# A gated hybrid decoder block: the root's scale and epsilon inside its square root, the last chunk squared on VectorE, one of the last four multiplications on GpSimd

## The chip, the cores and the metric

The kernel runs on one core of a Trainium2 chip. The metric is the device time of one execution in microseconds (us), given as the median of several runs; the kernel before has 1648.81 us as the median of three (1648.59 to 1650.45).

## The reference

One decoder block of width 2048 on 256 tokens, in float32. Three parts are added to the residual x one after the other, each on an RMS-normalised copy of it, and the result is normalised once more:

```python
def rms_norm(x, g):
    y = x * lax.rsqrt(jnp.mean(x * x, axis=-1, keepdims=True) + EPS)
    return y * g

x = x + hybrid_mixer(rms_norm(x, g_mix), w_in, ..., w_out)
x = x + memory_cross_attention(rms_norm(x, g_cross), rms_norm(mem, g_mem), w_cq, w_ckv, w_co)
x = x + conv_glu_ffn(rms_norm(x, g_ffn), w_up, conv_w, conv_b, w_down)
return rms_norm(x, g_final)
```

The mixer merges gated linear attention and causal pooling by sigmoid gates. Nearly all arithmetic is products of the 256 tokens with weight matrices (312 MB of weights are read). What matters here is the five times repeated `rsqrt(mean(x*x) + EPS)`: for the mixer's input, for the memory and the cross attention's input, for the feed-forward input, and for the output.

## The kernel before

Tokens lie along the free dimension, the 2048 channels as 16 chunks of 128 partitions. Each weight tile is loaded by SyncE's DMA queue into a `raw` buffer, cast by ScalarE into a high part `wh` (line 110), and VectorE writes the rest `wl` as the difference (line 110). TensorE then makes two products for each tile in three terms. Up to three units of weights are prepared ahead (`LOOK`), in five buffers for `wh`, five for `wl` and six for `raw`. A scheduler gives each engine a fixed order of instructions; `behind` and `issue_after` put a small step behind a named matmul. Engines wait for each other by semaphores; an engine that waits holds back all that is queued behind on it. In the lists of instructions, `[waits DVE_49]` means that the instruction waits for VectorE.

A norm is made in three steps. `Sum` adds up squares (`acc`). `cols` sums them over the partitions by a matmul with ones into a small PSUM tile `cps` and calls `root`, whose result `rc` is the reciprocal root with one Newton step. `rows` puts `rc` on a diagonal (`diag`) and spreads it over the partitions by another matmul (`rps`). The PSUM tiles `cps` and `rps` come from the pool `aux`, which has four buffers handed out in turn. The square root has its own table of ScalarE (the ACT_TABLE_LOAD in front of line 292).

At the start (mixer, values and decay gates) `va_unit` makes the products of lines 403 to 405. The units of the second half (n = 1) accumulate in four tiles of the pool `aux`: `va_0_560`, `va_1_561`, `va_0_562` and `va_1_563`. The tile `cps_mix` is allocated between the first tile of that pool (`warm`) and these four, so that the fourth of them, `va_1_563`, lies in the buffer of `cps_mix` and can be written when the last reader of `cps_mix` is done.

At the end, the last six chunks of the down projection are made for tokens 0 to 127 first (lines 922, 923), then for tokens 128 to 255 (line 928). `tail_out` adds the two halves of the product to x (line 891), squares on ScalarE (893), adds the square to `acc` on VectorE (896), and for the last chunk hands the square itself to `tail_norm`, which sums it by a matmul of its own (903). `tail_norm` makes the root, the diagonal (907), the spreading matmul (909), and then four multiplications of 128x512 on VectorE (912), each followed by its store on SyncE's queue (913). The first token half runs under the matmuls of the second; the second half is alone at the end.

Of the kernel before, what the change touches and what calls it, by code (L numbers as in the profile page):

```python
# [8 lines left out]
F32 = mybir.dt.float32  # L9
F32R = mybir.dt.float32r  # L10
U32 = mybir.dt.uint32
AF = mybir.ActivationFunctionType
# [3 lines left out]
P = 128  # L16
T = 256
D = 2048
NC = D // P
# [123 lines left out]
def block(ctx, tc, xT, memT, vecs, masks, wa2, wpool, w_va, w_in, w_branch, w_out, w_ckv_k, w_ckv_v, w_cq, w_co, w_up, w_down, out):  # L143
    nc = tc.nc
# [8 lines left out]
    sm = ctx.enter_context(tc.tile_pool(name="sm", bufs=2))  # L153
# [32 lines left out]
    def xc(c):  # L186
        return x[c // 4][:, c % 4, :]
# [23 lines left out]
    eps_t = const.tile([P, 1], F32, name="eps_t")  # L211
# [39 lines left out]
    class Sum:  # L251
# [18 lines left out]
        def cols(self):  # L270

            ps = aux.tile([P, 2], F32, tag="aux", name=f"cps_{self.name}")
            for t in range(2):
                nc.tensor.matmul(ps[:, t : t + 1], lhsT=self.acc[:, t * P : (t + 1) * P], rhs=ones[:, 0:1], start=True, stop=True)
            return root(ps, 2, self.name)
# [12 lines left out]
    def root(ps, n, name):  # L288

        v, y, z, r = (const.tile([P, n], F32, name=f"rc{i}_{name}") for i in range(4))  # L290
        nc.vector.tensor_scalar(v, ps, 1.0 / D, EPS, ALU.mult, ALU.add)
        nc.scalar.activation(y, v, AF.Sqrt)
        nc.vector.reciprocal(y, y)
        nc.vector.tensor_mul(z, y, y)
        nc.vector.scalar_tensor_tensor(z, z, -0.5, v, ALU.mult, ALU.mult)
        nc.vector.scalar_tensor_tensor(r, z, 1.5, y, ALU.add, ALU.mult)
        return r
# [13 lines left out]
    def gemm(unit, act, name, n=NC):  # L311

        ps = mm.tile([P, 2 * T], F32, tag="mm", name=f"ps_{name}")
        products(ps, terms(W.get(unit), act, n))
        return ps
# [27 lines left out]
    def total(ps, name):  # L343

        t = sm.tile([P, T], F32, tag="ev", name=f"ev_{name}", bufs=3)
        nc.scalar.copy(t, ps[:, T : 2 * T])
        u = sm.tile([P, T], F32, tag="eu", name=f"eu_{name}", bufs=3)
        nc.vector.tensor_add(u, ps[:, 0:T], t)
        return u
# [32 lines left out]
    v = [big.tile([P, HEADS, T], F32, tag="u", name=f"v{t}") for t in range(2)]  # L382
# [277 lines left out]
    for m in range(NC):  # L660
        wps = W.get(br0 + m)
        ys = []
        for n in (1, 0):
            ps = mm.tile([P, 2 * T], F32, tag="mm", name=f"br{m}_{n}")
            products(ps, [(wps[n], k, og if n == 0 else op, k) for k in range(8)])
            y = total(ps, f"br{m}_{n}")
# [32 lines left out]
    for m in range(NC):  # L699
        ps = gemm(ck0 + m, me, f"ck{m}")  # L700
# [170 lines left out]
    def scale_last(m, t=None):  # L871
        ts = slice(0, 2) if t is None else slice(t, t + 1)
        nc.scalar.activation(y_fin[m // 4][:, ts, m % 4, :], halves(xc(m))[:, ts, :], AF.Identity, scale=col(V_FINAL, m))
# [14 lines left out]
    def tail_out(m, t, ps):  # L888
        xt = xc(m)[:, t * P : (t + 1) * P]
        for g in range(2):  # L890
            nc.vector.tensor_add(xt, xt, ps[:, g * T + t * P : g * T + (t + 1) * P])
        sq = sm.tile([P, P], F32, tag="sq", name=f"sqt{m}_{t}", bufs=3)
        nc.scalar.activation(sq, xt, AF.Square)
        if m < NC - 1:
            a = s_z.acc[:, t * P : (t + 1) * P]
            nc.vector.tensor_add(a, a, sq)
            scale_last(m, t)
        return sq

    def tail_norm(t, sq):  # L900
        ps = aux.tile([P, 1], F32, tag="aux", name=f"cps_fin{t}")
        nc.tensor.matmul(ps, lhsT=s_z.acc[:, t * P : (t + 1) * P], rhs=ones[:, 0:1], start=True, stop=False)
        nc.tensor.matmul(ps, lhsT=sq, rhs=ones[:, 0:1], start=False, stop=True)
        rc = root(ps, 1, f"fin{t}")
        scale_last(NC - 1, t)
        diag = sm.tile([P, P], F32, tag="sq", name=f"diag_fin{t}", bufs=3)
        nc.vector.tensor_scalar(diag, ident, rc, None, ALU.mult)
        ps = aux.tile([P, P], F32, tag="aux", name=f"rps_fin{t}")
        nc.tensor.matmul(ps, lhsT=ones, rhs=diag, start=True, stop=True)
        for i in range(4):  # L910
            y = y_fin[i][:, t]
            nc.vector.tensor_mul(y, y, ps[:, None, :].to_broadcast([P, 4, P]))
            nc.sync.dma_start(out[t, :, 4 * i : 4 * i + 4, :], y)

    tails = []
    for m in range(NC - TAIL, NC):
        pool, tag = (aux, "aux") if m >= NC - 2 else (mm, "mm")
        ps = pool.tile([P, 2 * T], F32, tag=tag, name=f"ps_dt{m}")
        ts = terms(W.get(down0[2] + m), ga[2], n_last)
        products(ps, ts[:1], last=False)  # L920
        for (hi, lo), k, act, c in ts[1:]:
            nc.tensor.matmul(fours(ps[:, 0:T]), lhsT=lo[:, k * P : (k + 1) * P], rhs=fours(act.hi(c)), start=False, stop=False, skip_group_check=True)
            nc.tensor.matmul(of_tokens(ps, 0), lhsT=hi[:, k * P : (k + 1) * P], rhs=of_tokens(act.both(c), 0), start=False, stop=False, skip_group_check=True)
        sq = tail_out(m, 0, ps)
        tails.append((m, ps, ts))
    for n, (m, ps, ts) in enumerate(tails):
        for i, ((hi, lo), k, act, c) in enumerate(ts[1:]):
            pe["last"] = nc.tensor.matmul(of_tokens(ps, 1), lhsT=hi[:, k * P : (k + 1) * P], rhs=of_tokens(act.both(c), 1), start=False, stop=i == n_last - 2, skip_group_check=True)
        if n == 0:
            behind(tail_norm, 0, sq)  # L930
        sq1 = tail_out(m, 1, ps)
    tail_norm(1, sq1)


# [53 lines left out]
```

## Time and profile before

| | |
|---|---|
| median of 3 runs | 1648.81 us |
| profiled execution, its own time | 1650.06 us |
| its span in the profile | 1648.3 us |
| TensorE busy | 1635.4 us (99%) |
| VectorE busy | 1227.9 us (74%) |
| ScalarE busy | 899.4 us (55%) |
| GpSimd busy | 31.1 us (2%) |
| granted TensorE clock, mean | 0.998 |

The times in the rows below count from the span's start. The profiled execution took 1.76 us more than its span. PE is TensorE's matmuls, PEld its weight loads, DVE VectorE, ACT ScalarE, POOL GpSimd, SPq the issuing of DMAs on SyncE.

### The profile page before, as it was taken

Reading aid. Unit: us, or ns where it says so; the run is one execution under the profiler, and the core shown is the slowest. Engines: PE = TensorE matmul, PEld = TensorE weight load, DVE = VectorE, ACT = ScalarE, POOL = GpSimd, SP = SyncE. Lnnn points to the kernel's source line nnn. Section 1 sums busy time; section 2 is a strip of 40 time slices with the busy share of each in tenths; the row PEclk is TensorE's granted clock in tenths of the full one; section 3 lists DMA queues with packets and bytes.
Section 4 is the critical chain, followed back from the end, with each engine's and each line's share of the span. In section 5 each row is a group of like instructions: output and inputs, shape, how many; then the busy total and the mean of one; then the engine's idle time right before and its main releaser. Section 6 shows DMA issues by size and latency. Waiting matters only on the chain.

```text
span 1648.3 us, 26006 instructions
## 1 busy us (share of the span) xinstructions
PE 1635.4 (99%) x9900; PEld 1474.9 (89%) x9900; DVE 1227.9 (74%) x1906; ACT 899.4 (55%) x1376; POOL 31.1 (2%) x137
## 2 busy tenths in 40 slices
PE   8999999999999999999999999999999999999997
PEld 8999998989988898889999999999999999999987
DVE  7588768677888855447777788886678887678876
ACT  7555447445556644446555565654356664446563
POOL 2000000000001100000000000000000000000000
PEclk9999999999999999999999999999999999999999
DMA  8665556656666666665446666666666666666663
GB/s 275 208 200 171 168 166 189 218 169 201 195 220 210 196 199 196 192 194 177 154 144 199 194 195 200 196 200 196 199 196 198 198 196 200 195 201 194 180 183 109
DMA packets 90734, 316.15 MB, mean 192 GB/s; under 512 B 10208, under 2 KB 11104, under 8 KB 90608
## 3 DMA queue, kind: packets, MB, share of 16 engines
q1 hardware_dynamic: 90464, 314.43, 61.2%
q8 instruction: 77, 1.26, 0.3%
q14 instruction: 49, 0.40, 0.1%
q10 hardware_dynamic: 144, 0.05, 0.0%
HBM read 312.35 MB, written 2.10 MB: 191 GB/s over the span
## 4 chain that ended last, share of the span: by engine, by line
PE 97%; DMA 1%; DVE 1%; ACT 1%; issue 0%; SPq 0%; DVEq 0%; ACTq 0%
PE ps_up L329 19%; PE ps_up L330 10%; PE ps_g L329 7%; PE ps_dn L329 7%; PE ps_dn L330 4%; PE ps_g L330 4%; PE ps_wc L329 3%; PE ps_ck L329 3%; PE ps_cq L329 3%; PE br L329 3%; PE ps_wo L329 3%; PE ps_cq L330 2%; PE br L330 2%; PE ps_wc L330 2%; PE ps_ck L330 2%; PE cv L722 2%
## 5 line engine op out<-in xcount | busy, mean ns | idle before, releaser
L110 ACT CAST wh<-raw 128x1024 fp32r<-128x1024 f32 (+3 forms) x602 | 613.1, 1021 | 652.4 <-issue 204.1
L110 DVE TENSOR_TENSOR wl<-raw,wh 128x1024 fp32r<-128x1024 f32 (+3 forms) x602 | 718.2, 1195 | 331.9 <-ACT wh L110 322.2
L329 PE MATMUL ps_up<-h,wh 128*128 128x512 f32 x1408 | 469.9, 380 | 0.0
L330 PE MATMUL ps_up<-h,wl 128*128 128x256 f32 x1408 | 386.4, 274 | 0.0
L329 PEld LDWEIGHTS ps_up<-h,wh 128*128 128x128 f32 x1408 | 264.3, 188 | 45.3
L330 PEld LDWEIGHTS ps_up<-h,wl 128*128 128x128 f32 x1408 | 264.5, 188 | 0.0
L329 PE MATMUL ps_g<-h,wh 128*128 128x512 f32 x512 | 173.3, 384 | 0.0
L329 PE MATMUL ps_dn<-ga,wh 128*128 128x512 f32 x512 | 170.8, 380 | 0.0
L330 PE MATMUL ps_g<-h,wl 128*128 128x256 f32 x512 | 140.6, 275 | 0.0
L330 PE MATMUL ps_dn<-ga,wl 128*128 128x256 f32 x512 | 140.5, 274 | 0.0
L329 PEld LDWEIGHTS ps_g<-h,wh 128*128 128x128 f32 x512 | 96.2, 188 | 16.8 <-ACT wh L110 0.2
L329 PEld LDWEIGHTS ps_dn<-ga,wh 128*128 128x128 f32 x512 | 96.1, 188 | 16.5
L330 PEld LDWEIGHTS ps_g<-h,wl 128*128 128x128 f32 x512 | 96.2, 188 | 0.3 <-issue 0.2
L330 PEld LDWEIGHTS ps_dn<-ga,wl 128*128 128x128 f32 x512 | 96.2, 188 | 0.0
L329 PE MATMUL ps_wo<-mg,wh 128*128 128x512 f32 x256 | 87.2, 386 | 0.1
L329 PE MATMUL ps_cq<-h,wh 128*128 128x512 f32 x256 | 86.3, 382 | 0.0
L329 PE MATMUL ps_wc<-oc,wh 128*128 128x512 f32 x256 | 85.9, 381 | 0.0
L329 PE MATMUL ps_ck<-me,wh 128*128 128x512 f32 x256 | 85.9, 382 | 0.0
L330 PE MATMUL ps_wo<-mg,wl 128*128 128x256 f32 x256 | 70.4, 276 | 0.0
L330 PE MATMUL ps_ck<-me,wl 128*128 128x256 f32 x256 | 70.3, 274 | 0.0
L330 PE MATMUL ps_cq<-h,wl 128*128 128x256 f32 x256 | 70.3, 274 | 0.0
L330 PE MATMUL ps_wc<-oc,wl 128*128 128x256 f32 x256 | 70.1, 275 | 0.0
(322 smaller groups left out, 2747.2 us busy)
## 6 DMA issues: line engine op xcount, KB each, us to landing
raw<-w_up SPq DMA_DIRECT2D x176, 512.0 KB, 4.1
raw<-w_in SPq DMA_DIRECT2D x112, 512.0 KB, 3.9
raw<-w_down SPq DMA_DIRECT2D x64, 512.0 KB, 4.3
raw<-w_branch SPq DMA_DIRECT2D x32, 512.0 KB, 4.3
raw<-w_out SPq DMA_DIRECT2D x32, 512.0 KB, 4.1
raw<-w_ckv_k SPq DMA_DIRECT2D x32, 512.0 KB, 3.9
raw<-w_ckv_v SPq DMA_DIRECT2D x32, 512.0 KB, 4.3
raw<-w_cq SPq DMA_DIRECT2D x32, 512.0 KB, 4.4
```

The costliest lines, as they stand in the source:

```text
L110: return self.nc.scalar.copy(hi, src), self.nc.vector.tensor_sub(lo, src, hi.bitcast(F32))
L329: nc.tensor.matmul(fours(ps), lhsT=wh, rhs=fours(act.both(c)), start=f, stop=False, skip_group_check=True)
L330: pe["last"] = nc.tensor.matmul(fours(ps[:, 0:T]), lhsT=wl, rhs=fours(act.hi(c)), start=False, stop=l, skip_group_check=True)
L722: nc.tensor.matmul(fours(acc[t]), lhsT=xh, rhs=fours(wl), start=False, stop=False)
```

## The change

There are three edits.

In `root`, the square root reads the sums in PSUM directly, with the scale 1/D and the epsilon (the constant tile `eps_t`) as its own scale and bias. The value v = sum/D + EPS is still made on VectorE, since the Newton step needs it. `root` is called for all five norms.

In `tail_out`, the square of the last chunk (m = 15) is made on VectorE instead of ScalarE.

In `tail_norm`, ScalarE copies the spread factors `rps` from PSUM to a tile r in SBUF; GpSimd multiplies the first quarter of the output by r, and ScalarE's queue stores it; VectorE multiplies the other three quarters, the second one first, and SyncE's queue stores these.

```diff
     def root(ps, n, name):
         v, y, z, r = (const.tile([P, n], F32, name=f"rc{i}_{name}") for i in range(4))
+        nc.scalar.activation(y, ps, AF.Sqrt, bias=eps_t, scale=1.0 / D)
         nc.vector.tensor_scalar(v, ps, 1.0 / D, EPS, ALU.mult, ALU.add)
-        nc.scalar.activation(y, v, AF.Sqrt)
         nc.vector.reciprocal(y, y)
...
         sq = sm.tile([P, P], F32, tag="sq", name=f"sqt{m}_{t}", bufs=3)
-        nc.scalar.activation(sq, xt, AF.Square)
+        if m < NC - 1:
+            nc.scalar.activation(sq, xt, AF.Square)
+        else:
+            nc.vector.tensor_mul(sq, xt, xt)
...
-        for i in range(4):
+        r = sm.tile([P, P], F32, tag="eu", name=f"r_fin{t}", bufs=3)
+        nc.scalar.copy(r, ps)
+        for i in (1, 0, 2, 3):
             y = y_fin[i][:, t]
-            nc.vector.tensor_mul(y, y, ps[:, None, :].to_broadcast([P, 4, P]))
-            nc.sync.dma_start(out[t, :, 4 * i : 4 * i + 4, :], y)
+            by, eng, queue = (r, nc.gpsimd, nc.scalar) if i == 0 else (ps, nc.vector, nc.sync)
+            eng.tensor_mul(y, y, by[:, None, :].to_broadcast([P, 4, P]))
+            queue.dma_start(out[t, :, 4 * i : 4 * i + 4, :], y)
```

The edits change the order in which instructions stand. The first place is VectorE in the root of the mixer's norm. `wl_0_569` is the low part of a weight tile of the third unit of the second half; `rc_mix` stands for the four small tiles of the root, of which line 291 before and line 292 now write v.

```order
 L110 TENSOR_TENSOR wl_1_491<-raw_1_485,wh_1_490 128x780 [waits DMAHW5_49,PE_49,Activation_49]
-L291 TENSOR_SCALAR rc_mix<-cps_mix 128x2 [waits PE_49]
-L110 TENSOR_TENSOR wl_0_569<-raw_0_564,wh_0_568 128x780 [waits DMAHW0_49,Activation_49]
-L293 RECIPROCAL rc_mix<-rc_mix 128x2 [waits Activation_49]
+L110 TENSOR_TENSOR wl_0_569<-raw_0_564,wh_0_568 128x780 [waits DMAHW0_49,PE_49,Activation_49]
+L292 TENSOR_SCALAR rc_mix<-cps_mix 128x2 [waits Activation_49]
+L293 RECIPROCAL rc_mix<-rc_mix 128x2
```

The instruction that writes v stood in front of `wl_0_569` and waited for TensorE. It now stands behind it and waits for ScalarE, whose square root reads the same PSUM tile.

The second place is TensorE in the first unit of the second half, with the four accumulators named above.

```order
 L405 MATMUL va_0_562<-wl_0_453,h_147 128x260
-L403 MATMUL va_1_563<-wh_0_452,h_147 128x260 [waits DVE_49]
-L404 MATMUL va_1_563<-wh_0_452,h_147 128x260
-L405 MATMUL va_1_563<-wl_0_453,h_147 128x260
 L403 MATMUL va_0_560<-wh_0_452,h_147 128x260
...
 L405 MATMUL va_1_561<-wl_0_453,h_147 128x260
 L403 MATMUL va_0_562<-wh_1_454,h_147 128x260 [waits Activation_49]
+L403 MATMUL va_1_563<-wh_0_452,h_147 128x260 [waits DVE_49]
+L404 MATMUL va_1_563<-wh_0_452,h_147 128x260
+L405 MATMUL va_1_563<-wl_0_453,h_147 128x260
```

The three matmuls that first write `va_1_563` stand seven matmuls later than before (three on `va_0_560`, three on `va_1_561`, one on `va_0_562`). The first of them still waits for VectorE.

The third place is VectorE at the very end, in the second token half. `x_92` holds the last four chunks, `y_9549` to `y_9551` are the second to the fourth quarter of the output.

```order
+L899 TENSOR_TENSOR acc_fin<-acc_fin,sqt_1_16951 128x128 [waits Activation_49]
 L891 TENSOR_TENSOR x_92<-x_92,ps_dt_16813 128x128 [waits PE_49]
-L896 TENSOR_TENSOR acc_fin<-acc_fin,sqt_1_16949 128x128 [waits DVE_49,Activation_49]
 L891 TENSOR_TENSOR x_92<-x_92,ps_dt_16813 128x128 [waits DVE_49]
...
+L896 TENSOR_TENSOR sqt_1_16968<-x_92 128x128 [waits DVE_49]
+L292 TENSOR_SCALAR rc_fin_16973<-cps_fin_16970 128x1 [waits Activation_49]
+L293 RECIPROCAL rc_fin_16974<-rc_fin_16974 128x1
...
+L918 TENSOR_TENSOR y_9549<-y_9549,rps_fin_16986 128x512 [waits Activation_49]
+L918 TENSOR_TENSOR y_9550<-y_9550,rps_fin_16986 128x512
+L918 TENSOR_TENSOR y_9551<-y_9551,rps_fin_16986 128x512
```

The sum of chunk 14 stands before both additions of chunk 15 instead of between them, v is written after ScalarE's square root, and the first multiplication waits for ScalarE, which copies the same `rps` to r. Before, the first multiplication waited for TensorE alone.

## Rows read from the trace of the kernel before

**Rows 1.** Page, part 1: busy time of each engine, share, instructions

```profile
PE 1635.4 (99%) x9900; PEld 1474.9 (89%) x9900; DVE 1227.9 (74%) x1906; ACT 899.4 (55%) x1376; POOL 31.1 (2%) x137
```

**Rows 2.** Waits of TensorE: total us, times, longest

```profile
PE rps_fin L909 <- DVE diag_fin L907: 1.7, 1, 1.7
...
PE va L403 <- DVE rc_mix L291: 0.6, 1, 0.6
```

**Rows 3.** Windows: stretch, its length, busy PE PEld DVE ACT POOL, PEclk, DMA share, GB/s

```profile
36.00:1638.40 1602.40, 1602.32 (x9665) 1444.17 (x9663) 1196.39 (x1844) 872.42 (x1320) 21.65 (x105) 1.00 0.61 190
```

**Rows 4.** Timeline at the mixer's root: start us, duration us, engine, line, operation

```profile
33.68 0.28 PE L404 MATMUL va<-wh,h 128*128 128x260 f32 x1
33.80 0.28 PE L405 MATMUL va<-wl,h 128*128 128x260 f32 x1
34.46 0.15 DVE L291 TENSOR_SCALAR rc_mix<-cps_mix 128x2 f32<-128x2 f32 x1
...
34.67 0.39 PE L403 MATMUL va<-wh,h 128*128 128x260 f32 x1 [0.59 <-DVE rc_mix L291]
...
35.02 0.85 ACT L110 CAST wh<-raw 128x780 fp32r<-128x780 f32 x1 [1.81 <-DMA raw<-w_va]
...
35.89 1.28 ACT L292 ACT_TABLE_LOAD   x1
35.90 0.97 DVE L110 TENSOR_TENSOR wl<-raw,wh 128x780 fp32r<-128x780 f32 x1 [1.28 <-ACT wh L110]
...
37.18 0.20 ACT L292 ACTIVATE rc_mix<-rc_mix 128x2 f32<-128x2 f32 x1
```

**Rows 5.** Timeline at the feed-forward norm's root

```profile
940.16 1.23 DVE L110 TENSOR_TENSOR wl<-raw,wh 128x1024 fp32r<-128x1024 f32 x1 [0.19 <-ACT wh L110]
...
941.62 0.59 PE L283 MATMUL rps_wc<-diag_wc,ones 128*128 128x256 f32 x2
```

**Rows 6.** Timeline of the end

```profile
1638.45 0.29 DVE L891 TENSOR_TENSOR x<-x,ps_dt 128x128 f32<-128x128 f32 x1 [0.32 <-PE ps_dt L928]
...
1638.86 0.28 DVE L891 TENSOR_TENSOR x<-x,ps_dt 128x128 f32<-128x128 f32 x1
1639.24 0.31 ACT L893 ACTIVATE sqt<-x 128x128 f32<-128x128 f32 x1 [0.65 <-DVE x L891]
1639.60 0.38 PE L903 MATMUL cps_fin<-ones,sqt 128*128 128x1 f32 x2 [0.22 <-ACT sqt L893]
1640.02 0.16 DVE L291 TENSOR_SCALAR rc_fin<-cps_fin 128x1 f32<-128x1 f32 x1 [0.88 <-PE cps_fin L903]
1640.21 0.20 ACT L292 ACTIVATE rc_fin<-rc_fin 128x1 f32<-128x1 f32 x1 [0.37 <-DVE rc_fin L291]
1640.45 0.16 DVE L293 RECIPROCAL rc_fin<-rc_fin 128x1 f32<-128x1 f32 x1 [0.27 <-ACT rc_fin L292]
...
1642.16 2.48 DVE L912 TENSOR_TENSOR y<-y,rps_fin 128x512 f32<-128x512 f32 x4 [0.64 <-PE rps_fin L909]
1642.87 2.17 SPq L913 DMA_DIRECT2D out<-y  x4
```

**Rows 7.** Windows of the last stores and the clock

```profile
1638.40:1642.20 3.80, 1.24 (x7) 0.89 (x6) 1.82 (x10) 0.99 (x4) 0.00 (x0) 1.00 0.01 2
1642.60:1643.00 0.40, 0.00 (x0) 0.00 (x0) 0.40 (x2) 0.00 (x0) 0.00 (x0) 0.83 0.00 0
1643.40:1644.00 0.60, 0.00 (x0) 0.00 (x0) 0.60 (x3) 0.00 (x0) 0.00 (x0) 0.50 0.49 184
1644.00:1645.00 1.00, 0.00 (x0) 0.00 (x0) 0.64 (x2) 0.00 (x0) 0.00 (x0) 0.50 1.04 385
...
1646.00:1647.00 1.00, 0.00 (x0) 0.00 (x0) 0.00 (x0) 0.00 (x0) 0.00 (x0) 0.50 0.51 186
```

**Rows 8.** Groups of GpSimd by form: count, busy us, mean ns, idle before

```profile
L268 POOL TENSOR_TENSOR acc_mem<-acc_mem,sq_mem 128x256 f32<-128x256 f32 x15 | 12.6, 842 | 215.3 <-ACT sq_mem L260 215.3
```

**Rows 9.** Source line 346: count, duration ns min/median/max, first and last start

```profile
L346 ACT COPY ev_ck<-ps_ck x16: 353/366/370, 568.8 to 649.0; 128x256 f32<-128x256 f32 x16
```

## The prediction

> **What bounds the kernel now.** I read the page's busy shares first: TensorE is busy in 99% of the span [rows 1]. What an edit is worth therefore depends on whether it moves TensorE or the two ends of the program where TensorE is not full. The list of TensorE's waits says where these are [rows 2]: the longest is in the output's norm (1.7 us for the diagonal), and one of 0.6 us is at the start, where a value matmul waits for the VectorE instruction that writes v in the mixer's root. Between the two, the windows view has no hole: from 36.00 to 1638.40 us TensorE is busy for 1602.32 of 1602.40 us [rows 3]. So a delay of TensorE near 35 us is carried whole to the end, and an engine other than TensorE gains nothing between.
>
> The timeline of the start shows that 0.6 us [rows 4]. The last matmul ahead begins at 33.80 and lasts 0.28, v is written from 34.46 to 34.61, and TensorE goes on at 34.67. The reader is to see why: the accumulator `va_1_563` lies in the buffer of `cps_mix`, so its first matmul waits until `cps_mix` has been read. The same rows show ScalarE 2.5 us behind: its cast waits for a DMA until 35.02, the table load follows at 35.89, and the square root stands at 37.18 to 37.38.
>
> The timeline of the end [rows 6] is a chain without cover: the last addition to x, the square, the sum, v, the root, the diagonal, the spreading matmul, four multiplications, four stores. The windows show what ends last [rows 7]: the stores move at a DMA share of 1.04 and 385 GB/s once they run, and the busy share adds up to 0.49 x 0.6 + 1.04 + 1 + 0.51, about 2.8 us, from roughly 1643.7 to 1646.5. The four multiplications need 2.48 us, from 1642.16. So it is the first store, issued at 1642.87, that sets when the transfers end; the later ones arrive while the engines are full.
>
> **The root, at the start.** Removed: the wait of ScalarE for v. Added: `cps_mix` now has a second reader, the square root, and v stands behind it. In the order shown with the change, v waits for ScalarE and has moved behind a weight difference; the first matmul on `va_1_563` still waits for VectorE, that is for v. The square root cannot come earlier than in the trace: the cast (35.02, on a DMA), the table load and the root follow each other without a gap, and none of them waited for v. So the root ends at 37.38, v starts 0.04 later (as the reciprocal did behind the root at the end, 1640.41 to 1640.45 [rows 6]), ends at 37.57, and TensorE goes on 0.06 later (34.61 to 34.67 [rows 4]), at 37.63 instead of 34.67: 2.96 us. Against that stand seven matmuls that now go ahead of the waiting one, 0.12 us each by the spacing of the rows at 33.68 and 33.80: 0.84 us. The delay is 2.96 - 0.84 = 2.12 us. Queued behind the waiting matmul is all of TensorE's work; behind v on VectorE are the root's steps, which waited until 37.42 anyway, and then a weight difference, 0.2 us later. The cast into the buffer that `va_1_563` reads can be some 0.7 us late, less than TensorE itself. From below, if v ran right behind the weight difference (35.90 + 0.97 = 36.87) without waiting for ScalarE, the delay would be 1.6; from above, without help from the seven, 2.96. I take 2.12, which the rows give directly.
>
> No row of before shows ScalarE and VectorE reading one small PSUM tile, so no row shows what their order costs. The Trainium skill, "PSUM — Partial Sum Buffer", section "PSUM bank collisions raise a hardware error", says that two engines must not be in one PSUM bank at once, two readers included, and that software keeps them apart. By that rule the waits for ScalarE in the order are real and the sum stands; if the two could read side by side, the start would cost 1.6 us and the end nothing, and the sum would be 1.6. It speaks against this change at two places.
>
> **The root, elsewhere.** At the feed-forward norm the second diagonal half now stands behind a weight difference of 1.23 us that starts at 940.16 and ends at 941.39; 0.2 to 0.25 us more brings it to 941.6, and the matmul that reads it stands at 941.62 [rows 5]. Its cover is used up but not passed: 0, at most 0.1. The memory's place is alike.
>
> **The end.** The square on VectorE saves the way to ScalarE: it ended at 1639.55 and could end at 1638.86 + 0.28 + 0.04 + 0.29 = 1639.47 [rows 6]. But the sum of chunk 14, which ran between the two additions of chunk 15, now stands ahead of both, and if it comes late, they do. I take 0, between 0.3 saved and 0.2 lost.
>
> The root: before, v at 1640.02, root at 1640.21, reciprocal at 1640.45. After, root at 1640.02 to 1640.22, v at 1640.26, the reciprocal, independent of v, some 0.1 behind it: 1640.35, 0.1 earlier. Without v in the way it would be 0.2 earlier, and at worst 0.
>
> The multiplications: the first VectorE one waits for ScalarE's copy of `rps`. The trace has the copy at 128x256 out of PSUM with 366 ns [rows 9] and a 128x128 ScalarE operation with 0.31 us [rows 6]; with the hand-over of 0.05, the first multiplication begins 0.36 us later (0.25 to 0.4). Three multiplications take about 1.9 instead of 2.48, so VectorE's last one ends 0.24 earlier, which gains nothing, since the stores are late by then. GpSimd's one: 842 ns for 128x256 [rows 8] makes between 0.84 and 1.7 for twice the length; I take 1.5. It runs beside VectorE's three and its store, the last, comes at about 1.9 after the copy at the latest, while the stores ahead of it keep the engines full for 2.1 us from 0.8 after their first issue. It would count only past 2.7 us. In the first token half ScalarE's queue holds behind that store's wait the next square, needed some 3 us later: covered.
>
> So the first store is issued 0.36 - 0.1 = 0.26 later, and the end moves by 0.26. All four use the same bytes; whether a second queue helps is answered by the share of 1.04 with one queue [rows 7]. The Trainium skill, "DMA: Bandwidth & Descriptors", section "Issuing engines are not separate DMA queues", says the same: another issuing engine saves only issue time. If it did add rate, the last quarter (0.7 us) would lie beside the others and the end would gain 0.4 instead of losing 0.26.
>
> **The sum.** 2.12 + 0 + 0.26 = 2.4 us. The profiled execution has 1650.06 (span 1648.3 and 1.76 around it), so 1652.5 by its own time. The median of the runs is 1.25 below it, so 1648.81 + 2.4 = 1651.2. That is 0.14%; what the measurement can tell from no change is 0.2%, 3.3 us: up to 1652.1 counts as the same.
>
> **The rivals.** (a) The clock falls in the new hole: slower. TensorE would stand still for 2.7 us (34.92 to 37.63), against 0.6 before. The longest hole in the trace with the clock kept is 1.7 us [rows 2], and the granted clock stayed at 2.4 GHz through a stretch in which TensorE was busy for 1.24 of 3.8 us; it fell to 1.2 GHz about 0.7 us after the last matmul, behind that stretch [rows 7]. A hole of 2.7 us has not been seen, but full work stands on both sides of it. Price: the one stretch at the lower level in the trace lasts from about 1642.8 to 1648.3, 5.5 us; work through as long a stretch would lose half of it, 2.7. Total 5.1, 1653.9. It decides from a fall at about 37 us.
>
> (b) The start loses nothing: the accumulator gets another buffer, or v comes early enough. For it speaks that ScalarE is free in parts of 33 to 35 us; against it, that its rows there are tied to a DMA. Only the end's 0.26 would be left: 1649.1.
>
> (c) The change does what its three edits say and nothing else: 0.2 for the root's step, 0.1 for the square, 0.6 for the quarter less, no wait at the start: 1647.9. Against it stand the order (the wait for the copy) and the stores at their rate.
>
> **How the numbers follow.** The forecast gets 0.67, (a) 0.14, (b) 0.13, (c) 0.06. The forecast's own range is 1650.2 to 1652.4 (the start's 1.6 to 2.96, the end's -0.4 to 0.5, the spread of the runs); about a tenth of it lies above 1652.1. Slower: 0.14 + 0.07 = 0.21. Faster, below 1645.5: 0.02, from unknown causes alone. Same: 0.77. The range leaves out (c), half of (b) and half of (a): 1649.0 to 1653.6.
>
> **What would show it.** In the changed profile: TensorE waiting once, about 2.7 us, at line 403 for line 292 near 37.6 us; line 292 at the start behind the root at 37.4; the clock at full there or not; from 40 to 1638 no new hole; the first multiplication about 0.35 us behind the spreading matmul; GpSimd's multiplication between 0.84 and 1.7 us; the stores still at about 385 GB/s. It is wrong if TensorE's last matmul of line 928 (before, ending at about 1638.4) does not end about 2 us later.

## The result: 0.6% slower, in two groups of runs

The changed kernel took 1663.63 us in the median of 17 runs (1650.99 to 1667.69), the kernel before 1649.37 us in 17 runs of the same comparison (1648.42 to 1653.87). The ratio of the mean times is 1.0059, with a 95% interval from 1.0039 to 1.0078; the medians alone give 1.0086, since the median fell into the upper of two groups. That is slower, and outside the predicted range of 1649.0 to 1653.6.

The median hides what happened. The 17 runs fall into two groups with nothing between: 8 runs from 1650.99 to 1653.88 (median 1651.70) and 9 runs from 1663.63 to 1667.69 (median 1665.80). The lower group lies at the forecast: 1651.70 - 1649.37 = 2.33 us, where the sum said 2.4. Part of that is luck, as the account of the start will show. The upper group is 14 us above it, and nothing in the prediction speaks of 14 us.

The profiled execution took 1653.59 us (span 1651.8), so it belongs to the lower group. Its trace shows the predicted steps, but it cannot show the loss itself; that had to come from the experiments.

### The profile page after: what moved, and what is told of

Its sections match the earlier page's. It is cut to its first block, busy times and chain, and to the rows that moved or that the text cites. A ratio compares the mean times of both kernels' runs of the same rounds, so it can differ in the third digit from the quotient of the medians.

```text
span 1651.8 us, 26001 instructions
## 1 busy us (share of the span) xinstructions
PE 1636.9 (99%) x9900; PEld 1474.3 (89%) x9900; DVE 1227.4 (74%) x1906; ACT 901.4 (55%) x1376; POOL 33.6 (2%) x139
## 4 chain that ended last, share of the span: by engine, by line
PE 97%; DVE 1%; DMA 1%; ACT 1%; issue 0%; SPq 0%; DVEq 0%; ACTq 0%
PE ps_up L329 19%; PE ps_up L330 10%; PE ps_g L329 7%; PE ps_dn L329 7%; PE ps_g L330 4%; PE ps_dn L330 4%; PE ps_wc L329 3%; PE ps_ck L329 3%; PE ps_cq L329 3%; PE br L329 3%; PE ps_wo L329 3%; PE ps_wc L330 2%; PE ps_cq L330 2%; PE ps_ck L330 2%; PE br L330 2%; PE cv L721 2%
```

## The profile after

Busy time, in answer to [rows 1]; TensorE has 1.5 us more, GpSimd 2.5 us more for its two multiplications:

```profile
PE 1636.9 (99%) x9900; PEld 1474.3 (89%) x9900; DVE 1227.4 (74%) x1906; ACT 901.4 (55%) x1376; POOL 33.6 (2%) x139
```

TensorE's waits, in answer to [rows 2] (total us, times, longest). The wait for the mixer's root has grown from 0.6 to 2.4 us and is now TensorE's longest:

```profile
PE va L403 <- DVE rc_mix L292: 2.4, 1, 2.4
PE rps_fin L912 <- DVE diag_fin L910: 1.6, 1, 1.6
...
PE cps_fin L906 <- DVE sqt L896: 0.5, 1, 0.5
```

The timeline of the start, in answer to [rows 4] (start us, duration us, engine, line, operation, idle before and its releaser). Cast, table load, root and v follow each other, and TensorE goes on 0.05 us after v:

```profile
34.18 0.28 PE L403 MATMUL va<-wh,h 128*128 128x260 f32 x1
34.20 0.84 ACT L110 CAST wh<-raw 128x780 fp32r<-128x780 f32 x1 [2.70 <-DMA raw<-w_va]
35.06 1.28 ACT L291 ACT_TABLE_LOAD   x1
35.07 0.97 DVE L110 TENSOR_TENSOR wl<-raw,wh 128x780 fp32r<-128x780 f32 x1 [1.82 <-ACT wh L110]
36.35 0.26 ACT L291 ACTIVATE rc_mix<-cps_mix,eps_t 128x2 f32<-128x2 f32 x1
36.65 0.16 DVE L292 TENSOR_SCALAR rc_mix<-cps_mix 128x2 f32<-128x2 f32 x1 [0.60 <-ACT rc_mix L291]
...
36.86 0.39 PE L403 MATMUL va<-wh,h 128*128 128x260 f32 x1 [2.41 <-DVE rc_mix L292]
```

The feed-forward norm's spreading matmul, in answer to [rows 5]. The weight difference runs from 943.20 to 944.43; the second half of the diagonal follows until 944.63; the matmul in front of the spreading one begins at 944.55, and the spreading one at 944.68. That is 0.13 us later, where a start behind such a matmul usually follows after 0.11. The spreading one spans 0.70 us for its two instructions, where it spanned 0.59 before:

```profile
943.20 1.23 DVE L110 TENSOR_TENSOR wl<-raw,wh 128x1024 fp32r<-128x1024 f32 x1
...
944.35 0.28 DVE L282 TENSOR_SCALAR diag_wc<-ident,rc_wc 128x128 f32<-128x128 f32 x1
...
944.55 0.27 PE L330 MATMUL ps_up<-h,wl 128*128 128x256 f32 x1
944.68 0.70 PE L283 MATMUL rps_wc<-diag_wc,ones 128*128 128x256 f32 x2
```

So TensorE lost about 0.13 us here: 0.02 us ahead of the matmul and 0.11 us inside it. The list of waits does not show it; the duration does. This small delay turns out to be behind 12 of the 14 us of the upper group.

The memory's spreading matmul is held up in the same way, by 0.08 us inside its first instruction. Its instructions (duration ns min/median/max, first and last start us), before and after:

```profile
L283 PE MATMUL rps_mem<-diag_mem,ones x2: 377/378/379, 572.4 to 572.7; 128*128 128x256 f32 x2
```

```profile
L283 PE MATMUL rps_mem<-diag_mem,ones x2: 379/420/460, 573.8 to 574.1; 128*128 128x256 f32 x2
```

The end, in answer to [rows 6]:

```profile
1643.19 0.26 ACT L291 ACTIVATE rc_fin<-cps_fin,eps_t 128x1 f32<-128x1 f32 x1 [0.36 <-PE cps_fin L906]
1643.48 0.16 DVE L292 TENSOR_SCALAR rc_fin<-cps_fin 128x1 f32<-128x1 f32 x1 [0.77 <-ACT rc_fin L291]
1643.56 0.15 DVE L293 RECIPROCAL rc_fin<-rc_fin 128x1 f32<-128x1 f32 x1
...
1645.26 0.27 ACT L914 COPY r_fin<-rps_fin 128x128 f32<-128x128 f32 x1 [1.81 <-PE rps_fin L912]
1645.56 1.88 DVE L918 TENSOR_TENSOR y<-y,rps_fin 128x512 f32<-128x512 f32 x3 [0.94 <-ACT r_fin L914]
1645.60 1.27 POOL L918 TENSOR_TENSOR y<-y,r_fin 128x512 f32<-128x512 f32 x1 [7.16 <-ACT r_fin L914]
```

The copy takes 0.27 us, and VectorE's first multiplication begins 0.30 us behind the copy's start. GpSimd's multiplication takes 1.27 us and is done before VectorE's three. From the last matmul of the down projection to the last instruction it is 10.09 us, against 9.86 before: 0.23 longer. That last matmul ends at 1641.71 instead of 1638.42, which is 3.3 us later and not about 2; some 1.6 us of it are a slower pace of TensorE in the `ps_wc` stage, which the experiments explain. The windows of the stores (stretch, length, busy PE PEld DVE ACT POOL, PEclk, DMA share, GB/s) answer to [rows 7]; two queues move no more than one did:

```profile
1647.20:1648.20 1.00, 0.00 (x0) 0.00 (x0) 0.24 (x1) 0.00 (x0) 0.00 (x0) 0.50 1.01 375
1648.20:1649.20 1.00, 0.00 (x0) 0.00 (x0) 0.00 (x0) 0.00 (x0) 0.00 (x0) 0.50 1.03 385
```

## The experiments

Each was timed in five rounds beside the kernel before. Where an edit is one of the change's three, the first lines of it are shown. The experiments e1 to e8 ran on one chip, e9 and e10 on a second, e11 and e12 on a third.

### One edit at a time, and the change again

Two theories stood at first: that the upper group comes out of the start, where the hole leads to something longer (S), or out of the end, where GpSimd's multiplication or its store is late in some runs (G).

e1, the root alone:

```diff
+        nc.scalar.activation(y, ps, AF.Sqrt, bias=eps_t, scale=1.0 / D)
         nc.vector.tensor_scalar(v, ps, 1.0 / D, EPS, ALU.mult, ALU.add)
-        nc.scalar.activation(y, v, AF.Sqrt)
```

> Only the first edit: the square root reads the sums in PSUM with scale and epsilon of its own; square and multiplications as before. The changed kernel has two groups of runs, one about 2 us above before (1651 to 1654) and one about 15 us above (1663.6 to 1667.7). Theory S (the start: the hole of TensorE at line 403 sometimes sets off something longer, such as late weights): this kernel shows both groups, 1650.5 to 1653 and 1663 to 1668. Theory G (GpSimd's multiplication or ScalarE's store behind it is sometimes some 13 us late): this kernel has the first group alone, 1650.5 to 1652, that is before plus about 2 us, with TensorE waiting 2 to 2.7 us at line 403.

Measured: 1654.31 us, ratio 1.0040 (1.0021 to 1.0059). Of 12 runs 4 stand at 1662.2 to 1664.1, and 8 at 1649.6 to 1657.3: the upper group is there without the other two edits.

e2, the last chunk's square alone:

```diff
-        nc.scalar.activation(sq, xt, AF.Square)
+        if m < NC - 1:
+            nc.scalar.activation(sq, xt, AF.Square)
+        else:
+            nc.vector.tensor_mul(sq, xt, xt)
```

> Only the second edit: the last chunk squared on VectorE. Both theories: no upper group. The end's chain should move by 0 to 0.5 us, so 1648.4 to 1650.9, the same as before. An upper group here would refute both.

Measured: 1650.10 us, ratio 1.0001 (0.9992 to 1.0009); no upper group.

e3, the copy and GpSimd's multiplication alone:

```diff
+        r = sm.tile([P, P], F32, tag="eu", name=f"r_fin{t}", bufs=3)
+        nc.scalar.copy(r, ps)
+        for i in (1, 0, 2, 3):
+            by, eng, queue = (r, nc.gpsimd, nc.scalar) if i == 0 else (ps, nc.vector, nc.sync)
```

> Only the third edit: ScalarE's copy, GpSimd's multiplication of the first quarter, its store on ScalarE's queue. Theory G: both groups, about 1649 to 1650 and about 1661 to 1666 (before plus 12 to 16). Theory S: one group, 1648.5 to 1650.5, since the start is as before. Aside from the groups, my sum gives 0.36 us for the copy that VectorE waits for.

Measured: 1649.48 us, ratio 0.9999 (0.9990 to 1.0008); no upper group. G has fallen.

e4, all three edits again:

> The changed kernel itself once more, on this chip and beside the parts. Both theories: two groups again, 1651 to 1654 and 1663 to 1668, some six runs in ten in the upper one. If the profile falls in the upper group it shows the place: theory G expects the some 13 us between the copy to r and the end, in the first or second token half; theory S expects holes of TensorE between 37 us and the tail.

Measured: 1653.29 us, ratio 1.0026 (1.0010 to 1.0042); 10 runs from 1650.0 to 1654.3 and one at 1667.9. How often the upper group comes differs widely between two sets of runs of the same code (9 of 17, 1 of 11).

The profile of e1 fell into the upper group (1663.72 us), so it shows where the time is. Three windows views of the same 640 us of the feed-forward part, first the kernel before, then the changed kernel's profile, then e1:

```profile
950.00:1590.00 640.00, 640.00 (x3839) 577.89 (x3838) 497.38 (x749) 352.19 (x510) 8.32 (x84) 1.00 0.64 195
```

```profile
950.00:1590.00 640.00, 640.00 (x3840) 577.62 (x3839) 496.76 (x748) 353.20 (x510) 8.51 (x85) 1.00 0.64 195
```

```profile
950.00:1590.00 640.00, 640.00 (x3766) 568.38 (x3765) 487.30 (x731) 341.70 (x495) 8.42 (x84) 1.00 0.64 192
```

The reader is to see that TensorE is busy without a gap in all three, at the full granted clock (PEclk 1.00), and yet e1 makes 73 matmuls fewer. The work there is pairs of one 512-column and one 256-column matmul. A pair takes 640 / (3839 / 2) = 333.4 ns before and 339.9 ns in e1. The groups of lines show the same in their mean durations (busy us, mean ns), e1 first, then before:

```profile
L329 PE MATMUL ps_up<-h,wh 128*128 128x512 f32 x1408 | 479.0, 386 | 0.0
...
L329 PE MATMUL ps_dn<-ga,wh 128*128 128x512 f32 x512 | 174.2, 386 | 0.0
```

```profile
L329 PE MATMUL ps_up<-h,wh 128*128 128x512 f32 x1408 | 469.9, 380 | 0.0
...
L329 PE MATMUL ps_dn<-ga,wh 128*128 128x512 f32 x512 | 170.8, 380 | 0.0
...
L329 PE MATMUL ps_wo<-mg,wh 128*128 128x512 f32 x256 | 87.2, 386 | 0.1
L329 PE MATMUL ps_wc<-oc,wh 128*128 128x512 f32 x256 | 85.9, 381 | 0.0
```

So TensorE has two steady paces for this work, told apart by 380 to 382 or 386 ns. From the spreading matmul of the feed-forward norm to the output's norm it is 689.39 us before, 689.51 in the changed kernel's profile and 701.48 in e1: 12.1 us. The last two rows show that the kernel before has both paces too: its `ps_wo` stage ran at the slow one and its `ps_wc` stage at the fast one, where 256 pairs make 1.7 us of difference. In the changed kernel's profile `ps_wc` is slow as well (386 ns; the stage has 99.26 us against 97.64). S is right that the root brings the group, but its place was wrong: e1's slow pace does not begin at the start. It begins right behind the spreading matmul of the feed-forward norm.

The start times of the matmuls show where a pace begins and ends. In all fourteen profiles, every change of pace that lasts eight pairs or more stands at a place where another order breaks the alternation of 512 and 256 columns: other matmuls between the pairs, or two matmuls of the same width one after the other. Between two such places the pace holds. Behind the feed-forward norm's spreading matmul the next such place is some 1900 pairs away, in the `ps_dl` stage, at 1577.40 us before and 1591.73 in e1. There the two kernels change over, the kernel before to the slow pace and e1 to the fast one. The windows (as above) ahead of it and behind it, the kernel before first, then e1:

```profile
1546.00:1576.00 30.00, 30.00 (x182) 27.10 (x181) 24.78 (x42) 17.30 (x30) 0.40 (x4) 1.00 0.54 152
1579.00:1609.00 30.00, 30.00 (x179) 26.65 (x178) 22.43 (x39) 18.90 (x33) 0.00 (x0) 1.00 0.67 199
```

```profile
1560.00:1590.00 30.00, 30.00 (x178) 26.65 (x177) 24.29 (x42) 16.61 (x29) 0.40 (x4) 1.00 0.54 147
1593.00:1623.00 30.00, 30.00 (x182) 27.09 (x182) 22.85 (x40) 19.12 (x33) 0.00 (x0) 1.00 0.70 202
```

So the slow pace is nothing that the change brought. What is special at the feed-forward norm is that the pace taken there lasts for 1900 pairs.

### Is it the feed-forward norm's wait, or the start?

Theory P: the short wait of TensorE at that spreading matmul puts it into the slow pace in some runs. Theory H: the hole at the start does it. Three kernels put the new root at some norms only (`name` is the norm), and one leaves the root as it was and makes the diagonal late by other means.

e5, the whole change, but the old root at the feed-forward norm ("wc"):

```diff
+        if name != "wc":
+            nc.scalar.activation(y, ps, AF.Sqrt, bias=eps_t, scale=1.0 / D)
+            nc.vector.tensor_scalar(v, ps, 1.0 / D, EPS, ALU.mult, ALU.add)
+        else:
             nc.vector.tensor_scalar(v, ps, 1.0 / D, EPS, ALU.mult, ALU.add)
             nc.scalar.activation(y, v, AF.Sqrt)
```

> The whole change, but the feed-forward norm (wc) keeps the old root. In the upper group's profile TensorE waits 0.13 us at the spreading matmul of that norm and then runs each pair of matmuls of the feed-forward part at 340 instead of 333.5 ns. Theory P (that short wait throws TensorE out of step, and the pace in which it comes back lasts for some 2000 pairs, 12 to 14 us): without the late diagonal no run above 1656; 1650.5 to 1654. Theory H (the hole at the start, with or without the fall of the clock, is what leads to the slow pace later): still some runs at 1662 to 1668.

Measured: 1651.92 us, ratio 1.0015 (1.0007 to 1.0024); 11 runs from 1649.26 to 1654.14, none in the upper group.

e6, the new root at the feed-forward norm alone (`if name == "wc"`), nothing else of the change:

> Only the feed-forward norm has the new root; all else is the kernel before, so no hole at the start. Theory P: two groups, 1648 to 1651 and 1660 to 1665, or runs spread between the two. Theory H: 1647.5 to 1651 alone.

Measured: 1651.83 us, ratio 1.0030 (1.0011 to 1.0049); 4 of 12 runs at 1660.7 to 1661.5, the others from 1648.98 to 1652.8. The upper group needs neither the start's hole nor the end's edits. This is the cleanest comparison of all: the matmuls of e6 stand in the order of the kernel before, one for one, and what e6 adds on TensorE is the delay at the spreading matmul. The kernel before first, then e6:

```profile
L283 PE MATMUL rps_wc<-diag_wc,ones x2: 378/378/378, 941.6 to 941.8; 128*128 128x256 f32 x2
```

```profile
L283 PE MATMUL rps_wc<-diag_wc,ones x2: 379/431/483, 940.6 to 940.9; 128*128 128x256 f32 x2
```

The profile of e6 is of a run at 1649.11 us: with the same delay TensorE took the fast pace that time.

e7, the new root at the mixer's norm alone (`if name == "mix"`):

> Only the mixer's norm at the start has the new root. Both theories share the price of the hole: 1.8 to 2.2 us where the clock stays, some 2 us more where it falls: 1650 to 1654. Theory P: nothing above 1656. Theory H: a part of the runs at 1661 to 1666.

Measured: 1651.02 us, ratio 1.0012 (1.0003 to 1.0020); 1648.73 to 1653.37, no upper group. H has fallen.

e8, no edit of the change; at the feed-forward norm the second diagonal half is made from a copy of the identity that a 128x512 multiplication on VectorE holds back:

```diff
+            own = ident
+            if self.name == "wc":
+                own = big.tile([P, 512], F32, tag="u", name="own")
...
+                for _ in range(1):
+                    nc.vector.tensor_mul(own, own, own)
-                nc.vector.tensor_scalar(diag[:, t * P : (t + 1) * P], ident, rc[:, t : t + 1], None, ALU.mult)
+                nc.vector.tensor_scalar(diag[:, t * P : (t + 1) * P], (ident, own[:, 0:P])[t], rc[:, t : t + 1], None, ALU.mult)
```

> No edit of the change at all: in the kernel before, the second half of the feed-forward diagonal is built from a copy of the identity that one VectorE multiplication of 128x512 has gone over (it leaves zeros and ones as they are), so that it stands behind a weight difference and comes some 0.1 to 0.2 us late, as in the changed kernel. Theory P, if it is the wait and not the root: two groups or a spread, 1648 to 1651 and up to 1665. If it needs the new root in some other way: 1647.5 to 1651 alone.

Measured: 1660.98 us, ratio 1.0058 (1.0036 to 1.0079); 5 of 6 runs at 1660.64 to 1661.77, one at 1649.01. The part behind the spreading matmul takes 701.24 us. With the old root everywhere, a late half brings the upper group, so it is not the root itself. One thing differs besides: the spreading matmul of e8 stands inside a pair, behind the 512-column matmul, where the kernels so far have it between two pairs, and no run has that place without a delay. Taken with e6, where the place is that of the kernel before, P holds. The delay is 0.08 us here. The spreading matmuls (duration ns min/median/max) and the windows of the feed-forward part of e8:

```profile
L291 PE MATMUL rps_wc<-diag_wc,ones x2: 379/414/449, 940.4 to 940.6; 128*128 128x256 f32 x2
```

```profile
950.00:1590.00 640.00, 640.00 (x3765) 568.20 (x3765) 486.83 (x730) 340.75 (x493) 8.42 (x84) 1.00 0.64 192
```

### A longer wait, the wait taken away, and the end alone

e9, the new root at the output's norm alone and the square on VectorE:

```diff
+        if name[:3] == "fin":
+            nc.scalar.activation(y, ps, AF.Sqrt, bias=eps_t, scale=1.0 / D)
...
+            nc.vector.tensor_mul(sq, xt, xt)
```

> The new root at the output's norm alone and the square of the last chunk on VectorE; the other four roots as before, the four multiplications as before. Theory P (the loss comes from the start's hole and from the short wait at the feed-forward norm, and neither is here): no run in the upper group (1660 or more), the part behind the feed-forward norm 689.4 us, the part behind the last matmul 9.7 us (before 9.86; the root alone gave 9.79, the square alone 9.75), so 0.1 to 0.3 us below the kernel before, about 1649.2: not to be told from it. The rival (the new root costs something wherever it stands): 0.3 us or more above the kernel before.

Measured: 1648.93 us, ratio 0.9992 (0.9983 to 1.0001), 1646.91 to 1650.07. The part behind the last matmul takes 9.71 us instead of 9.86. As expected; it cannot be told from the kernel before.

e10, as e8, with two of those multiplications (`for _ in range(2)`):

> The kernel before with two multiplications of 128x512 on VectorE ahead of the second diagonal half at the feed-forward norm, where the experiment before had one: TensorE waits there for about 0.7 us instead of 0.1. Theory P1 (any wait of TensorE at this place lets the pace of the following part fall out by chance, whatever its length): some runs, between 2 and 8 of 10, some 12 us above the others, as with 0.1 us. Rival P2 (only a wait as short as 0.1 us puts the stream out of step; a longer one starts it anew): no run above 1655, all 0.6 to 0.9 us above the kernel before. Either way the time shows in the part between the spreading matmul and the output's norm, 690 or 702 us.

Measured: 1649.32 us, ratio 0.9998 (0.9989 to 1.0007), 11 runs from 1648.41 to 1650.81, none in the upper group.

```profile
L291 PE MATMUL rps_wc<-diag_wc,ones x2: 379/431/483, 941.3 to 941.6; 128*128 128x256 f32 x2
```

The experiment missed its aim: the scheduler put the spreading matmul four matmuls later, so the wait did not grow to 0.7 us; the durations are those of the new root, 379/431/483. What it does show is that a wait of this size at a slightly different place, and on another chip, led to the slow pace in 0 of 11 runs. The wait makes the slow pace possible behind this matmul, and something else decides.

e11, the new root at the feed-forward norm alone, as e6, but its diagonal in one instruction, which stands whole ahead of the weight difference:

```diff
+            if self.name == "wc":
+                nc.vector.tensor_mul(diag[:, :].rearrange("p (t c) -> p t c", t=2), ident[:, None, :].to_broadcast([P, 2, P]), rc[:, :, None].to_broadcast([P, 2, P]))
+            else:
```

> The new root at the feed-forward norm alone, as in e6, but the diagonal there is written by one VectorE instruction of 128x256 instead of two of 128x128; in the order it stands whole ahead of the weight difference of 1.23 us that parted the two halves in e6. Theory W (the upper group comes from TensorE's short wait at the spreading matmul, not from the new root): the first spreading matmul has 377 to 378 ns again and both stand 215 ns apart, no run stands in the upper group (1660 or more) where e6 had 4 of 12, about 1649.4, not to be told from the kernel before. Rival R (the new root at this place brings the group by itself, or by what else it moves on VectorE and ScalarE): 2 to 8 of 12 runs about 12 us above the others, as in e6.

Measured: 1649.44 us, ratio 1.0000 (0.9991 to 1.0009); 11 runs from 1648.77 to 1650.67. The matmuls stand in the order of e6. The one instruction takes 0.43 us, and the wait is gone:

```profile
L286 PE MATMUL rps_wc<-diag_wc,ones x2: 377/378/378, 941.1 to 941.3; 128*128 128x256 f32 x2
```

e12, the whole change with that diagonal:

> The whole change with the feed-forward norm's diagonal in one instruction, so without the short wait there. Theory W: the start's 1.8 us with or without the fall of the clock (up to 1.7 more) and the end's 0.2 stay, the upper group goes: 1651 to 1652, none of the runs at 1660 or more, as when the whole change was run with the old root at that norm (1651.92). Rival R: some runs at 1663 or more, as in the changed kernel (9 of 17).

Measured: 1653.42 us, ratio 1.0024 (1.0015 to 1.0032); 11 runs from 1649.77 to 1655.05. The upper group is gone, as theory W has it; the median is 1.4 us above the expectation's 1652, and 4.4 us above its kernel before. Taken together: with the new root at this norm and the parted diagonal, 18 of 52 runs were in the upper group (9 of 17 of the changed kernel, 4 of 12 of e1, 1 of 11 of e4, 4 of 12 of e6); with the new root and the diagonal in one instruction, none of 22. Those 22 ran on a chip on which no kernel with the wait was run, so they are not proof by themselves. On the chip of e1 to e8 alone, the kernels with the wait at this norm (e1, e4, e6, e8) were in the upper group in 14 of 41 runs, and those without it (e2, e3, e5, e7 and the kernel before) in none of 108.

## Why the prediction was wrong, step by step

**The root, at the start: right in its path, on the average too small.** TensorE waits 2.41 us at line 403 for line 292, against 0.59: 1.82 us more, where the forecast had 2.12 (1.6 to 2.96). The path is the one named: the cast waits for its DMA, the table load and the root follow, v stands behind the root. The terms were alike too: the seven matmuls go ahead, and v came 0.04 us behind the root's end (36.61 to 36.65). What varies is when the DMA lets the cast go; the wait is 2.6 us in e1 and e4, 1.8 in e5 and e12, 1.3 in e7. The kernel before varies there too, and its one trace, from which the sum was made, was not typical. From the sums to the spreading matmul of the mixer's norm it took 14.26 us, and 14.30 in e11; in the other six profiles with the old root at that norm (e2, e3, e6, e8, e9, e10) it took 13.43 to 13.49, and TensorE did not wait for v there. With the new root it took from 14.99 (e7) to 17.84 us (e1). The means of the eight and the six profiles are 2.85 us apart, of which falls of the clock (below) are a part. So the 2.33 us of the lower group come near the forecast partly by luck; e4 and e12, with the same start, have medians 3.7 and 4.4 us above the kernel before.

The Trainium skill, "PSUM — Partial Sum Buffer", section "PSUM bank collisions raise a hardware error", has two engines kept apart on one bank by software. The traces agree as far as the order goes: v waited for ScalarE here and at the end (1643.45 to 1643.48). What two readers at once would do, no run here shows.

**The root, elsewhere: this step failed.** It said: "Its cover is used up but not passed: 0, at most 0.1." The delay itself was near enough, 0.13 us. What was wrong is that a delay of TensorE costs its own length and no more. e6 and e8 show that this one costs 12 us in some runs, because TensorE falls into its slower pace for the pairs of the up and the down projection behind it (1376 and 512, each some 6.5 ns longer: 12.3 us), and in e5, e11 and e12, without the delay at this norm, no run has the loss. The memory's place was called alike, and it was: its delay of 0.08 us is in the five profiles with the new root there (the changed kernel's, e1, e4, e5, e12). In all five TensorE went on at the fast pace behind it; what it cost in runs that were only timed is not shown.

**The end: right, on thin evidence.** 0.23 us longer, where 0.26 was forecast. One profile of each kernel is little for that: in e10 and e11, whose end is that of the kernel before, it took 10.14 and 10.15 us instead of 9.86. There the granted clock was already at 0.50, the 1.2 GHz level, at the output's spreading matmul, which took 0.76 and 0.77 us instead of 0.46 for its two instructions. The parts: the square and the root together gain 0.15 (e9), the copy with GpSimd loses 0.30 (e3: 10.16 us against 9.86). GpSimd's multiplication took 1.27 us where 1.5 was taken, and its store did not end last. The Trainium skill, "DMA: Bandwidth & Descriptors", section "Issuing engines are not separate DMA queues", says that another issuing engine saves issue time alone, and so spoke against a gain from the second queue; the stores at 375 to 385 GB/s agree.

**The rivals.** (a) was half right and wrongly placed as an alternative. Behind the hole the granted clock fell to half, the 1.2 GHz level, in three of the six profiles that have it (e1, e4, e5; not in the changed kernel's, e7 or e12). In e1, by windows:

```profile
37.00:38.00 1.00, 0.88 (x7) 0.88 (x8) 0.86 (x7) 0.34 (x1) 0.00 (x0) 1.00 0.83 212
38.00:39.00 1.00, 1.00 (x8) 1.00 (x8) 0.70 (x3) 1.00 (x3) 0.00 (x0) 0.67 0.45 171
39.00:40.00 1.00, 1.00 (x6) 1.00 (x6) 0.91 (x4) 0.98 (x3) 0.00 (x0) 0.50 0.00 0
```

Its price is read from two kernels with the same wait of 1.8 us, e5 with the fall and e12 without, in the same stretch:

```profile
37.00:41.00 4.00, 4.00 (x24) 4.00 (x23) 2.39 (x9) 3.16 (x6) 0.00 (x0) 0.61 0.50 156
```

```profile
37.00:41.00 4.00, 4.00 (x36) 4.00 (x35) 2.89 (x8) 2.80 (x7) 0.00 (x0) 1.00 0.44 135
```

Twelve matmuls fewer at 0.12 us are 1.4 us; from the sums to the spreading matmul of the mixer's norm it is 17.05 us in e5 and 15.47 in e12, 1.6 us. The forecast's 2.7 was too much, since the clock came back after about 3.4 us (in e1 from 38.34 to 41.74, by the windows' means) and not 5.5. Wait and fall do not go by length alone: it fell behind 1.8 us in e5 and not behind 2.4 in the changed kernel's profile. (b) and (c) are out: the start lost 1.8 us.

**The chances.** The forecast had 0.77 on no measurable change and 0.21 on slower, all of the latter from the clock and the upper edge of the sum. No case had a delay with an effect larger than itself, although the kernel before showed two paces, and so a reason to ask what sets them: 386 ns for `ps_wo` beside 381 for `ps_wc`, the same work on the same shapes.

**What stays open.** What the slow pace is, and what picks it where the alternation is broken, is not shown: clock, DMA share and weight loads are alike, the same code does the one or the other from run to run, and e10's wait never led to it. The upper group of the changed kernel stands 14.1 us above the lower, of which the pace explains 12.1. The remaining 2 are of the size of a fall of the clock (1.6) or of another stage at the slow pace (1.7), as is e12's 1.4, but the runs that were only timed have no trace to show it, and the profile of e12 is its fastest run. Whether the upper group comes as often on every chip, no run here shows.

## What to carry to other kernels

Where TensorE streams without a gap, look at every place where its next operand comes just in time: a delay of 0.1 us there cost a hundred times as much in some runs here. Make the small chain that feeds such a matmul whole, with no large instruction between its parts (here one diagonal instruction instead of two), before asking what an edit saves. Take the wait that a sum starts from out of more than one profile of the kernel before; here six of eight did not have it. And when two stages of the same shapes have different mean durations in the groups of lines, count the runs by groups, since a median can land in either.

## What the runs showed of the hardware

- TensorE has two steady paces for pairs of a 512-column and a 256-column matmul at the full granted clock: 333.4 and 339.9 ns for a pair, 380 and 386 ns in the mean duration of the first. In the fourteen profiles a pace changes only where the alternation of the two is broken, and holds up to the next such place, for some 640 us behind the feed-forward norm.
- A stop of TensorE of 1.8 to 2.6 us between full work was followed by a fall of the granted clock to half in three of five profiles (once of 1.3 us: no fall), about 3.4 us long, at a price of 1.6 us (from one pair of profiles).
- A square root on ScalarE takes 0.26 us out of PSUM with a scale and a bias tile, and 0.20 us out of SBUF without them [rows 4], for the same two columns. Which of the two differences makes the 0.06 us, no run here shows.
